# Second expert layer: where the gate product is read, where the overflow branch stands, and how the last norm is formed

## The chip, the cores and the metric

The kernel runs on one core of a Trainium2 chip, as one program. The metric is the time of the whole program in microseconds (us) on the device, as the median of three runs. Beside the runs there is one execution that the hardware profiler recorded; its trace is what the rows below come from. Engines are named as the profile names them: PE is TensorE (matmuls), PEld its weight loads, DVE VectorE, ACT ScalarE, POOL GpSimd, SP SyncE. SPq, POOLq and so on are the sequencers that issue DMAs.

## The reference, cut to what matters

The program is two transformer blocks on 256 tokens of width 1024. The change touches the last part of the second block, a layer of eight experts with a layer norm behind it:

```python
def _moe_swiglu(u, w_router, w_gate, w_up, w_down):      # u: 256 x 1024, 8 experts, top 2, inner width 2816
    ...
    h = silu(ragged_dot(xs, w_gate, group_sizes)) * ragged_dot(xs, w_up, group_sizes)
    ys = ragged_dot(h, w_down, group_sizes) * top_w[order]
    return segment_sum(ys, tok, num_segments=n_tok)

# second_block, layer 1
ff = _moe_swiglu(u, ...)
x = _layernorm(DEEPNORM_ALPHA * x + (1.0 + g2) * ff, ln2_g, ln2_b)   # the program's output
```

All weights and products are float32.

## The kernel before, in words

The program is written as a list of jobs that run in one order; each engine's instructions stand in the order in which the jobs record them. Semaphores between engines are set by the framework, tile by tile.

**Experts and slots.** `second_moe` visits the eight experts in the order 0, 5, 1, 2, 6, 3, 4, 7. `CAP` gives each a fixed number of token slots: 96 for experts 0 to 4, and 64 for 5, 6 and 7. So the second, fifth and eighth experts visited have 64 slots, and expert 7, the last, is one of them. Slots 0 to 63 are "part 0", slots 64 to 95 "part 1" (only where `CAP` is 96). The tokens of an expert are gathered with matmuls against a matrix of zeros and ones (`np`) into `nX`.

**Chunks.** An expert's inner width of 2816 is taken in six chunks (`c` = 0 to 5), five of 512 and one of 256. In each chunk, for each part, `proj_jobs` multiplies `nX` first with the gate weights (key "g2") and then with the up weights ("u2"). Both products lie side by side in one PSUM tile, `box[part]`, which is one bank. ACT takes silu of the gate half into `ns` (L1864), DVE multiplies it by the up half into `nH` (L1866). Then `down_jobs` multiplies the chunk before ("d2", from `nHT` into the accumulators `acc`), and only after that `turn` transposes this chunk's `nH` on TensorE (L286) and copies it to `nHT` (L1883). So the down product of one chunk is done between the projections and the transposes of the next. An expert's finished sums are weighted, spread back to the tokens by matmuls (`combine`, `rest`) and added to `x` by DVE while the next expert runs.

**Weights.** Each weight tile is 1 MB (128 partitions x 2048 floats). 264 of them are needed in this layer, and there are 14 slots for them. SP issues all their loads in the order of first use (L166); a load waits until TensorE has finished with the tile that held its slot before. SP is one queue: whatever stands ahead of a load holds it up.

**Overflow branch.** `many` handles tokens beyond the fixed slots. It begins with a branch on a count that every engine loads (L1031, L1032), SP included, and jumps over a long body when the count is zero, as it is in these runs. It is job `J(many)`; before, it stands in the last expert visited (`x == NE2 - 1`) at chunk 3, ahead of that chunk's `turn`. A similar branch stands in the first block's expert layer, at about 260 us.

**End.** `end` weights the last expert's sums (`nyA`, L1933), spreads them to the tokens by four matmuls into four PSUM banks, adds them to `x` in SBUF (L2092), and makes the layer norm of the two halves of the tokens (`x0`, `x1`): statistics on DVE (L310), square root on ACT, then scale and shift, shared by ACT, DVE and POOL for `x0` and done by DVE alone for `x1`. Four DMAs write the output. The rows of norm weights are broadcast by two POOL DMAs of 0.5 MB into the tile `nrow`, which shares its memory with a tile of the overflow body.

Of the kernel before, what the change touches and what calls it, by code (L numbers as in the profile page):

```python
# [15 lines left out]
AF = mybir.ActivationFunctionType  # L16
OP = mybir.AluOpType
AX = mybir.AxisListType

P = 128  # L20
SEQ = 256
D = 1024
KD = D // P
# [5 lines left out]
NE2 = 8  # L29
C2 = 128  # L30
FF2 = 2816
ALPHA = 4.0 ** 0.25
RMS_EPS = 1e-6
LN_EPS = 1e-5
# [76 lines left out]
class Build:  # L111
# [192 lines left out]

    def stats(self, x):

        n = x.shape[1] // 512
        st = self.sm([P, n, 6], "bn_st")
        for i in range(n):
            self.nc.vector.bn_stats(st[:, i, :], x[:, i * 512:(i + 1) * 512])  # L310
        return st

    def deviation(self, st, eps, rms):
# [1381 lines left out]
    def second_moe(self):  # L1695
        nc, I, J = self.nc, self.I, self.job
# [141 lines left out]
        def proj_jobs(p, c, box, part):  # L1838

            n = min(512, FF2 - c * 512)  # L1840
            nj, fw, nq = 2048 // n, n // 2, n // P
            m, at, w = (nq, 32, P) if part else (2, 64, fw)
            stride = P if part else 256
            for a, key in enumerate(("g2", "u2")):
                for half in range(KD // nj):
                    def run(t, a=a, half=half):
                        X = place[p]["X"][:, :, 64:96] if part else place[p]["X"][:, :, 0:64]
                        w3 = t.rearrange("p (j n) -> p j n", n=n)
                        if a == half == 0:
                            box[part] = self.ps()  # L1850
                        for jj in range(nj):
                            j = half * nj + jj
                            for q in range(m):
                                self.mm(box[part][at * q:at * q + at, a * stride:a * stride + w], X[:, j, :],
                                        w3[:, jj, q * w:(q + 1) * w], j == 0, j == KD - 1)
                        if half < KD // nj - 1:
                            return
                        if "H" not in box:
                            box["s"] = self.t([P, 384], "ns", bufs=2)
                            box["H"] = self.t([P, 384], "nH", bufs=2)  # L1860
                        r, dst = slice(0, at * m), slice(256, 384) if part else slice(0, fw)
                        src = box[part][r, a * stride:a * stride + w]
                        if a == 0:
                            nc.scalar.activation(box["s"][r, dst], src, AF.Silu)  # L1864
                        else:
                            nc.vector.tensor_mul(box["H"][r, dst], box["s"][r, dst], src)  # L1866

                    J(run, (key, p, c, half))

# [65 lines left out]
                                               op1=OP.mult)  # L1935
            eb["y"] = y

        def combined(p, eb):

            y, PT = eb["y"][0], eb["PT"]  # L1940
            out = [[self.ps("acc") for _ in range(2)], [self.ps() for _ in range(2)]]
            for t in range(2):
                for dh in range(2):
                    r = slice(64 * dh, 64 * dh + 64)
                    self.mm(out[t][dh], PT[r, 0, t * P:(t + 1) * P], y[r, :], True, True)
            return out

        def combine(p, eb):
            def run():
                out = combined(p, eb)  # L1950
                for t in range(2):
                    for h in range(2):
                        dst = self.x[t][:, h * 512:(h + 1) * 512]
                        nc.vector.tensor_add(dst, dst, out[t][h])

            def rest():

                out = [self.ps() for _ in range(4)]
                y, PT = eb["y"][1], eb["PT"]
                for t in range(2):  # L1960
                    for dq in range(4):
                        r = slice(32 * dq, 32 * dq + 32)
                        self.mm(out[dq][:, t * 256:(t + 1) * 256], PT[r, 1, t * P:(t + 1) * P], y[r, :], True, True)
                for dq in range(4):
                    for t in range(2):
                        dst = self.x[t][:, dq * 256:(dq + 1) * 256]
                        nc.vector.tensor_add(dst, dst, out[dq][:, t * 256:(t + 1) * 256])

            J(run)
            return rest  # L1970

        def many():
            def body(e, rk, w):
# [51 lines left out]
        for p in ORDER:  # L2025
            for c in range(NC):
                n = min(512, FF2 - c * 512)
# [15 lines left out]
        for x, p in enumerate(ORDER):  # L2043
            eb = {}
            for c in range(NC):
                box = {}

                for part in (0, 1) if kind == 0 else (1, 0):
                    if part == 0 or CAP[p] > 64:
                        proj_jobs(p, c, box, part)  # L2050
                        kind = part
                    if x == c == 0 and part == 0:
                        J(by_tokens)
                        J(lambda: self.settled(lambda _, c: c > 9))
                        J(spread_gate)
                    if prev is not None and (part == 0 or CAP[prev[0]] > 64):
                        down_jobs(*prev, part)
                        kind = part
                if x == NE2 - 1 and c == 3:
                    J(many)  # L2060
                if prev is not None and prev[0] != p:
                    J(lambda a=prev: self.chain.append(lambda: weighted(a[0], a[3])))
                    waiting = prev
                turn(p, c, box)
                if c == 0:
                    weights_of_slots(p, eb)
                if c == 1 and waiting is not None:
                    rest = combine(waiting[0], waiting[3])
                    waiting = rest if CAP[waiting[0]] > 64 else None
                if c == 2 and waiting is not None:  # L2070
                    J(waiting)
                    waiting = None
                if c == 3 and x < NE2 - 1:
                    J(lambda b=ORDER[x + 1]: self.chain.extend([lambda: places(b), lambda: None] + gather(b)))
                prev = (p, c, box, eb)
        down_jobs(*prev, 0)

        def end(p=prev[0], eb=prev[3]):

            half = [slice(h * 512, (h + 1) * 512) for h in range(2)]  # L2080
            r = self.t([P, 2, D], "nrow", tag="nrows")
# [1 line left out]
            self.bcast_row(rg, I["ln2_g_2"][1:2, :])  # L2083
            self.bcast_row(rb, I["ln2_b_2"][1:2, :])
            weighted(p, eb)
            ps = combined(p, eb)
            mv, r = self.t([P, 2, 2], "e_mv"), self.t([P, 2], "e_r")
            b = self.t([P, 1], "e_b")

            def added(t):  # L2090
                for h in range(2):
                    nc.vector.tensor_add(self.x[t][:, half[h]], self.x[t][:, half[h]], ps[t][h])  # L2092

            def moments(t):
                st = self.stats(self.x[t])
                nc.vector.bn_aggr(mv[:, t, :], st.rearrange("p a b -> p (a b)"))  # L2096
                nc.vector.tensor_scalar_add(r[:, t:t + 1], mv[:, t, 1:2], LN_EPS / ALPHA ** 2)  # L2097
                nc.scalar.activation(r[:, t:t + 1], r[:, t:t + 1], AF.Sqrt)

            x0, x1 = self.x  # L2100
            added(0)
            moments(0)
            added(1)
            nc.vector.reciprocal(r[:, 0:1], r[:, 0:1])
            nc.vector.scalar_tensor_tensor(out=b, in0=mv[:, 0, 0:1], scalar=-1.0, in1=r[:, 0:1], op0=OP.mult, op1=OP.mult)  # L2105
            for h in range(2):
                nc.scalar.activation(x0[:, half[h]], x0[:, half[h]], AF.Identity, scale=r[:, 0:1], bias=b)  # L2107
            moments(1)
            for h in range(2):
                nc.vector.tensor_mul(x0[:, half[h]], x0[:, half[h]], rg[:, half[h]])  # L2110
                nc.gpsimd.tensor_add(x0[:, half[h]], x0[:, half[h]], rb[:, half[h]])
                nc.sync.dma_start(self.out[0, 0:P, half[h]], x0[:, half[h]])
            nc.vector.reciprocal(r[:, 1:2], r[:, 1:2])
            for h in range(2):
                nc.vector.scalar_tensor_tensor(out=x1[:, half[h]], in0=x1[:, half[h]], scalar=mv[:, 1, 0:1],  # L2115
                                               in1=rg[:, half[h]], op0=OP.subtract, op1=OP.mult)
                nc.vector.scalar_tensor_tensor(out=x1[:, half[h]], in0=x1[:, half[h]], scalar=r[:, 1:2],  # L2117
                                               in1=rb[:, half[h]], op0=OP.mult, op1=OP.add)
                nc.scalar.dma_start(self.out[0, P:2 * P, half[h]], x1[:, half[h]])

        J(end)

# [34 lines left out]
```

## Time and profile before

| what | value |
|---|---|
| three runs | 2068.54, 2069.56, 2069.57 us; median 2069.56 us |
| the profiled execution: its own time, its span in the trace | 2069.82 us, 2068.1 us |
| TensorE busy over the span | 1881.0 us (91%) |
| DVE, ACT, POOL busy | 662.2 us (32%), 443.0 us (21%), 106.6 us (5%) |
| granted TensorE clock, mean over the span | 0.973 of full speed |
| read from HBM | 655.30 MB |

The second expert layer's matmuls run from about 1280 us to 2051 us, more than a third of the span; the norm and the output take the last 17 us. "Busy" of an engine counts its own instructions, not its waits. An idle stretch of an engine is given in square brackets with the event that ended it.

### The profile page before, as it was taken

To read this page: it belongs to the slowest core of one execution; us is meant where nothing else is said; L and a number is where in the kernel's file an instruction comes from. 1 tells how busy PE (TensorE), PEld (TensorE's weight loads), DVE (VectorE), ACT (ScalarE), POOL (GpSimd) and SP (SyncE) were. 2 spreads that over 40 slices of the span, in tenths; PEclk is the share of its full clock that TensorE was granted. 3 is DMA by queue.
4 is the path that set the end of the run, shared out by engine and by line. 5 is a ranking of instruction groups with operands and counts; after the bars stand their busy time and mean duration, and the time that the engine had idled before them with its cause. 6 is when DMAs were issued, how large, how long until landed. Compare 5 with 4: busy or idle time off the path is not lost. (4 is left out here: it accounts for less than half of the span.)

```text
span 2068.1 us, 42041 instructions
## 1 busy us (share of the span) xinstructions
PE 1881.0 (91%) x18649; PEld 1333.2 (64%) x18650; DVE 662.2 (32%) x1201; ACT 443.0 (21%) x718; POOL 106.6 (5%) x97
## 2 busy tenths in 40 slices
PE   4999889999999979989998998999999999999995
PEld 2989655555554548979996896665556555565652
DVE  6454621122211235655455564202110111111112
ACT  4544410000001024444343442000000000000000
POOL 7020200000000000000000001000000000000000
PEclk9999999999999999989998998999999999999998
DMA  9759989999999999357737846899999889998894
GB/s 369 291 212 315 347 304 386 394 393 393 393 395 394 393 379 368 123 184 266 264 122 255 315 146 243 296 346 391 392 368 346 326 329 390 393 384 305 315 394 160
DMA packets 293665, 660.78 MB, mean 320 GB/s; under 512 B 11320, under 2 KB 30928, under 8 KB 293216
## 3 DMA queue, kind: packets, MB, share of 16 engines
q1 hardware_dynamic: 290864, 648.46, 84.9%
q0 software_dynamic: 2320, 8.97, 1.1%
q8 instruction: 152, 2.49, 0.5%
q10 hardware_dynamic: 288, 0.52, 0.1%
q14 instruction: 41, 0.34, 0.0%
HBM read 655.30 MB, written 2.62 MB: 318 GB/s over the span
## 5 line engine op out<-in xcount | busy, mean ns | idle before, releaser
L289 PE MATMUL mm<-w,nX 128*32 128x128 f32 (+2 forms) x6592 | 446.7, 317 | 38.1 <-ACT ns L1864 32.3
L289 PEld LDWEIGHTS mm<-w,nX 128*32 128x32 f32 (+1 forms) x6592 | 307.1, 123 | 176.8 <-ACT ns L1864 57.6
L204 DVE TENSOR_TENSOR wh<-w,wh 128x1024 fp32r<-128x1024 f32 x178 | 222.6, 1257 | 171.2 <-ACT wh L208 166.8
L289 PE MATMUL mm<-w,mxt 128*64 128x256 f32 x2048 | 235.5, 383 | 21.9 <-ACT msg L1251 17.5
L289 PEld LDWEIGHTS mm<-w,mxt 128*64 128x64 f32 x2048 | 145.5, 138 | 119.6 <-ACT msg L1251 32.1
L289 PE MATMUL acc<-w,nHT 128*32 128x256 f32 (+1 forms) x1584 | 215.1, 474 | 2.5 <-issue 2.0
L208 ACT ACTIVATE wh<-w 128x1024 fp32r<-128x1024 f32 x178 | 184.6, 1043 | 103.8 <-PE acc L289 65.3
L289 PE MATMUL mm<-uh,wh 128*128 128x256 f32 (+1 forms) x1376 | 194.5, 292 | 11.7 <-ACT uh L302 8.9
L289 PEld LDWEIGHTS mm<-uh,wh 128*128 128x128 f32 (+1 forms) x1376 | 178.1, 196 | 18.6 <-ACT uh L302 12.3
L1866 DVE TENSOR_TENSOR nH<-ns,mm 128x256 f32<-128x256 f32 (+2 forms) x78 | 27.7, 356 | 467.4 <-PE mm L289 461.4
L1864 ACT ACTIVATE ns<-mm 128x256 f32<-128x256 f32 (+2 forms) x78 | 25.8, 331 | 638.3 <-PE mm L289 638.3
L289 PEld LDWEIGHTS acc<-w,nHT 128*32 128x32 f32 (+1 forms) x1584 | 79.5, 122 | 98.9 <-issue 78.8
L289 PE MATMUL mm<-w,mHT 128*64 128x512 f32 x512 | 116.9, 598 | 13.2 <-DVE mHT L1278 13.2
L289 PE MATMUL mm<-ul,wh 128*128 128x256 f32 (+1 forms) x688 | 101.2, 292 | 0.0
L289 PEld LDWEIGHTS mm<-ul,wh 128*128 128x128 f32 (+1 forms) x688 | 92.1, 197 | 1.1
L289 PEld LDWEIGHTS mm<-w,mHT 128*64 128x64 f32 x512 | 33.9, 136 | 74.9 <-issue 53.4
L1254 DVE TENSOR_TENSOR mH<-msg,mm 128x256 f32<-128x256 f32 x32 | 13.5, 421 | 206.2 <-PE mm L289 206.2
L289 PE MATMUL mm<-hh,wh 128*128 128x256 f32 x416 | 60.7, 296 | 7.4 <-ACT wh L208 6.7
L1296 DVE SCALAR_TENSOR_TENSOR mYl<-mm,mws,mYh 128x512 fp32r<-128x512 f32 x32 | 24.0, 751 | 135.2 <-ACT mYh L1295 135.2
L1295 ACT ACTIVATE mYh<-mm,mws 128x512 fp32r<-128x512 f32 x32 | 22.0, 687 | 201.0 <-PE mm L289 201.0
L289 PEld LDWEIGHTS mm<-hh,wh 128*128 128x128 f32 x416 | 55.7, 202 | 9.6 <-ACT wh L208 7.2
L357 POOL TENSOR_TENSOR x<-x,sv 128x512 f32<-128x512 f32 x10 | 12.6, 1277 | 840.6 <-DVE sv L356 840.6
(423 smaller groups left out, 1901.7 us busy)
## 6 DMA issues: line engine op xcount, KB each, us to landing
w<-in_moe_w_gate_dram SPq DMA_DIRECT2D x88, 1024.0 KB, 12.8
w<-in_moe_w_up_dram SPq DMA_DIRECT2D x88, 1024.0 KB, 13.6
w<-in_moe_w_down_dram SPq DMA_DIRECT2D x88, 1024.0 KB, 12.5
w<-in_w_gate_dram SPq DMA_DIRECT2D x64, 1024.0 KB, 15.3
w<-in_w_up_dram SPq DMA_DIRECT2D x64, 1024.0 KB, 14.6
w<-in_w_down_dram SPq DMA_DIRECT2D x64, 1024.0 KB, 14.0
w<-in_ada_w_dram SPq DMA_DIRECT2D x24, 2048.0 KB, 10.3
w<-in_w_in_dram SPq DMA_DIRECT2D x19, 2048.0 KB, 15.2
```

The lines of the kernel that those rows point to most:

```text
L204: nc.vector.tensor_sub(lo, src, hi.bitcast(F32))
L208: nc.scalar.activation(shaped(hi), src, AF.Copy)
L289: self.nc.tensor.matmul(out, lhsT=lhsT, rhs=rhs, start=start, stop=stop)
L357: nc.gpsimd.tensor_add(self.x[1][:, sl[h]], self.x[1][:, sl[h]], y[h])
L1254: nc.vector.tensor_mul(H, box["s"], ps[:, 256:512])
L1295: nc.scalar.activation(Yh, ps, AF.Copy, scale=box["ws"])
L1296: nc.vector.scalar_tensor_tensor(out=Yl, in0=ps, scalar=box["ws"], in1=Yh.bitcast(F32), op0=OP.mult, op1=OP.subtract)
L1864: nc.scalar.activation(box["s"][r, dst], src, AF.Silu)
L1866: nc.vector.tensor_mul(box["H"][r, dst], box["s"][r, dst], src)
```

## The change

Three edits, all in or behind the second expert layer.

1. In `proj_jobs`, silu of the gate product is no longer recorded after the gate's last matmul but after the up product's last matmul, just ahead of the multiplication.
2. `J(many)`, the overflow branch, moves from the eighth expert visited, chunk 3, to the fifth, chunk 4; in both it stands ahead of the chunk's `turn`.
3. A new job `carried`, after the eighth expert's chunk 3, multiplies `x` by the identity into the four PSUM banks that `end` will use. The last matmuls then add on top of it in PSUM (`start` false), so that the four additions in SBUF fall away; statistics and the first step of the norm read PSUM, and the second half of the tokens takes the same path as the first. POOL's two additions go to DVE.

```diff
     def stats(self, x):
-        n = x.shape[1] // 512
-        st = self.sm([P, n, 6], "bn_st")
-        for i in range(n):
-            self.nc.vector.bn_stats(st[:, i, :], x[:, i * 512:(i + 1) * 512])
+        if not isinstance(x, list):
+            x = [x[:, i * 512:(i + 1) * 512] for i in range(x.shape[1] // 512)]
+        st = self.sm([P, len(x), 6], "bn_st")
+        for i, h in enumerate(x):
+            self.nc.vector.bn_stats(st[:, i, :], h)
         return st
...
-                        if half < KD // nj - 1:
+                        if a == 0 or half < KD // nj - 1:
                             return
...
-                        src = box[part][r, a * stride:a * stride + w]
-                        if a == 0:
-                            nc.scalar.activation(box["s"][r, dst], src, AF.Silu)
-                        else:
-                            nc.vector.tensor_mul(box["H"][r, dst], box["s"][r, dst], src)
+                        gate, up = (box[part][r, b * stride:b * stride + w] for b in range(2))
+                        nc.scalar.activation(box["s"][r, dst], gate, AF.Silu)
+                        nc.vector.tensor_mul(box["H"][r, dst], box["s"][r, dst], up)
...
+        def banks():
+            return [[self.ps("acc") for _ in range(2)], [self.ps() for _ in range(2)]]
+
-        def combined(p, eb):
+        def combined(p, eb, out, start):
             y, PT = eb["y"][0], eb["PT"]
-            out = [[self.ps("acc") for _ in range(2)], [self.ps() for _ in range(2)]]
             for t in range(2):
                 for dh in range(2):
                     r = slice(64 * dh, 64 * dh + 64)
-                    self.mm(out[t][dh], PT[r, 0, t * P:(t + 1) * P], y[r, :], True, True)
-            return out
+                    self.mm(out[t][dh], PT[r, 0, t * P:(t + 1) * P], y[r, :], start, True)
...
+        def carried():
+            self.xs = banks()
+            for t in range(2):
+                for h in range(2):
+                    self.mm(self.xs[t][h], self.ident, self.x[t][:, h * 512:(h + 1) * 512], True, False)
...
-                if x == NE2 - 1 and c == 3:
+                if x == 4 and c == 4:
                     J(many)
...
+                if x == NE2 - 1 and c == 3:
+                    J(carried)
                 prev = (p, c, box, eb)
...
             weighted(p, eb)
-            ps = combined(p, eb)
...
+            xs = self.xs
+            combined(p, eb, xs, False)
+            first = self.deviation(self.stats(xs[0]), LN_EPS / ALPHA ** 2, False)
+            st = self.stats(xs[1])
+            moments = [first, None]
+            for t in range(2):
+                if t == 1:
+                    moments[1] = self.deviation(st, LN_EPS / ALPHA ** 2, False)
+                mv, r = moments[t]
+                nc.vector.reciprocal(r, r)
+                b = self.sm([P, 1], "bn_b")
+                nc.vector.scalar_tensor_tensor(out=b, in0=mv[:, 0:1], scalar=-1.0, in1=r, op0=OP.mult, op1=OP.mult)
                 for h in range(2):
-                    nc.vector.tensor_add(self.x[t][:, half[h]], self.x[t][:, half[h]], ps[t][h])
...
+                    x = self.x[t][:, half[h]]
+                    nc.scalar.activation(x, xs[t][h], AF.Identity, scale=r, bias=b)
+            for t in range(2):
+                for h in range(2):
+                    x = self.x[t][:, half[h]]
+                    nc.vector.tensor_mul(x, x, rg[:, half[h]])
+                    nc.vector.tensor_add(x, x, rb[:, half[h]])
+                    (nc.sync, nc.scalar)[t].dma_start(self.out[0, t * P:(t + 1) * P, half[h]], x)
```

TensorE's rows in the last expert's chunk 4, before the change, with the semaphores that each row waits for (`DMAHW` is a weight tile's landing, `Activation` is ACT). The rows with `w,nX` are the two gate tiles, then the two up tiles; those with `w,nHT` are the down product of chunk 3; L286 is `turn`.

```order
L289 MATMUL mm<-w,nX 64x256 [waits DMAHW6_49,PE_49,Activation_49]
L289 MATMUL mm<-w,nX 64x256 x7
L289 MATMUL mm<-w,nX 64x256 [waits DMAHW7_49]
L289 MATMUL mm<-w,nX 64x256 x7
L289 MATMUL mm<-w,nX 64x256 [waits DMAHW0_49,Activation_49]
L289 MATMUL mm<-w,nX 64x256 x7
L289 MATMUL mm<-w,nX 64x256 [waits DMAHW1_49]
L289 MATMUL mm<-w,nX 64x256 x7
L289 MATMUL acc<-w,nHT 64x512 [waits DMAHW2_49,DVE_49]
```

The same place after the change, with the two pairs of identity matmuls ahead of the gate.

```order
L289 MATMUL acc<-x_81,cst 128x512 x2
L289 MATMUL mm<-x_82,cst 128x512 x2
L289 MATMUL mm<-w,nX 64x256 [waits DMAHW6_49,Activation_49]
L289 MATMUL mm<-w,nX 64x256 x7
L289 MATMUL mm<-w,nX 64x256 [waits DMAHW7_49]
L289 MATMUL mm<-w,nX 64x256 x7
L289 MATMUL mm<-w,nX 64x256 [waits DMAHW0_49]
L289 MATMUL mm<-w,nX 64x256 x7
L289 MATMUL mm<-w,nX 64x256 [waits DMAHW1_49]
L289 MATMUL mm<-w,nX 64x256 x7
L289 MATMUL acc<-w,nHT 64x512 [waits DMAHW2_49,DVE_49]
```

The wait for ACT at the first up tile is gone; the one at the first gate tile stays. The matmuls of `carried` wait for nothing.

SP's queue around the branch, before the change: the last three weight loads, and behind them the branch (its body, not taken, is left out).

```order
L166 DMA w<-in_moe_w_down_dram 128x2x1024
L166 ISA
L166 DMA w<-in_moe_w_down_dram 128x2x1024
L166 ISA
L166 DMA w<-in_moe_w_down_dram 128x2x1024
L1031 TENSOR_LOAD rt_mi
L1031 ISA x2
L1032 COMPARE_AND_BRANCH
```

SP's queue after the change, the rows where the branch is left and the loads go on (behind its skipped body):

```order
L1035 COMPARE_AND_BRANCH
L1035 UNCONDITIONAL_BRANCH
L1033 UNCONDITIONAL_BRANCH
L166 ISA
L166 DMA w<-in_moe_w_down_dram 128x2x1024
L166 ISA
L166 DMA w<-in_moe_w_gate_dram 128x4x512
```

Before, no load stands behind the branch; now 90 of the 264 do. The first of them is the second down tile of the sixth expert's chunk 0.

## Rows read from the trace of the kernel before

**Rows 1.** Windows, fifth expert: stretch, its length, engines' busy us, clock, DMA share, GB/s.

```profile
1680.00:1753.00 73.00, 70.20 (x564) 39.36 (x563) 13.58 (x36) 4.30 (x11) 0.00 (x0) 1.00 1.04 390
```

**Rows 2.** Waits of PE from 1280.5 to 2050.9: total us, times, longest.

```profile
PE mm L289 <- ACT ns L1864: 32.3, 71, 1.5
PE mm L286 <- PEq L1032: 4.4, 1, 4.4
```

**Rows 3.** Timeline, last expert, chunk 2: start, us, engine, line, operation, records, idle before.

```profile
1993.83 3.67 PE L289 MATMUL mm<-w,nX 128*64 128x256 f32 x32
...
1997.55 0.38 ACT L1864 ACTIVATE ns<-mm 128x256 f32<-128x256 f32 x1 [13.10 <-PE mm L289]
...
1997.99 3.67 PE L289 MATMUL mm<-w,nX 128*64 128x256 f32 x32 [0.48 <-ACT ns L1864]
...
2001.49 3.60 PE L289 MATMUL acc<-w,nHT 128*64 128x512 f32 x16
2001.78 0.42 DVE L1866 TENSOR_TENSOR nH<-ns,mm 128x256 f32<-128x256 f32 x1 [6.23 <-PE mm L289]
```

**Rows 4.** Timeline, sixth expert, chunk 0: `turn` of part 1, and the next down product.

```profile
1767.30 0.29 DVE L1866 TENSOR_TENSOR nH<-ns,mm 128x128 f32<-128x128 f32 x1 [5.92 <-PE mm L286]
...
1767.64 0.33 PE L286 MATMUL mm<-cst,nH 128*128 128x128 f32 x1 [0.48 <-DVE nH L1866]
...
1773.26 1.91 PE L289 MATMUL acc<-w,nHT 128*32 128x256 f32 x32
```

**Rows 5.** Landing time of single loads, issued at 1368.89, 1465.60 and 1758.34 us.

```profile
w<-in_moe_w_down_dram SPq DMA_DIRECT2D x1, 1024.0 KB, 4.9
...
w<-in_moe_w_down_dram SPq DMA_DIRECT2D x1, 1024.0 KB, 13.7
...
w<-in_moe_w_down_dram SPq DMA_DIRECT2D x1, 1024.0 KB, 14.4
```

**Rows 6.** Timeline: single load issues, and the third expert's first down product.

```profile
1465.60 1.03 SPq L166 DMA_DIRECT2D w<-in_moe_w_down_dram  x1
...
1661.47 0.92 SPq L166 DMA_DIRECT2D w<-in_moe_w_gate_dram  x1
...
1758.34 1.02 SPq L166 DMA_DIRECT2D w<-in_moe_w_down_dram  x1
...
1481.18 1.47 PE L289 MATMUL acc<-w,nHT 128*32 128x256 f32 x22
```

**Rows 7.** Timeline of PE around the overflow branch, last expert, chunks 3 and 4.

```profile
2015.20 3.60 PE L289 MATMUL acc<-w,nHT 128*64 128x512 f32 x16
...
2023.69 2.82 PE L289 MATMUL mm<-w,nX 128*64 128x256 f32 x11
...
2036.63 3.60 PE L289 MATMUL acc<-w,nHT 128*64 128x512 f32 x16
...
2040.53 1.97 PE L289 MATMUL mm<-w,nX 128*64 128x128 f32 x32
```

**Rows 8.** Timeline of PE behind the first block's branch.

```profile
268.15 5.36 PE L289 MATMUL mm<-w,mxt 128*64 128x256 f32 x32 [4.19 <-DVEq L1032]
```

**Rows 9.** SP's waits from 2015 to 2040, then from 255 to 270.

```profile
SPq L1032 <- SPq L1032: 13.8, 2, 8.5
...
SPq L1032 <- SPq L1032: 5.0, 1, 5.0
```

**Rows 10.** Timeline of the end: additions, statistics, scaling, last steps.

```profile
2052.87 1.28 DVE L2092 TENSOR_TENSOR x<-x,acc 128x512 f32<-128x512 f32 x2 [1.22 <-PE acc L289]
2054.07 1.28 DVE L310 BATCH_NORM_STATS2 bn_st<-x 128x6 f32<-128x512 f32 x2
...
2057.28 1.52 ACT L2107 ACTIVATE x<-x,e_b,e_r 128x512 f32<-128x512 f32 x2 [1.26 <-DVE e_b L2105]
...
2058.80 1.29 DVE L2110 TENSOR_TENSOR x<-x,nrow 128x512 f32<-128x512 f32 x2
...
2064.13 0.75 DVE L2117 SCALAR_TENSOR_TENSOR x<-x,e_r,nrow 128x512 f32<-128x512 f32 x1
```

More of the change, by code (lines that the diff above doesn't have):

```diff
@@ L1944, in combined @@
                     r = slice(64 * dh, 64 * dh + 64)
-                    self.mm(out[t][dh], PT[r, 0, t * P:(t + 1) * P], y[r, :], True, True)
-            return out
+                    self.mm(out[t][dh], PT[r, 0, t * P:(t + 1) * P], y[r, :], start, True)
         def combine(p, eb):
             def run():
-                out = combined(p, eb)
+                out = banks()
+                combined(p, eb, out, True)
                 for t in range(2):
@@ L2085, in end @@
             weighted(p, eb)
-            ps = combined(p, eb)
-            mv, r = self.t([P, 2, 2], "e_mv"), self.t([P, 2], "e_r")
-            b = self.t([P, 1], "e_b")
-            def added(t):
-                for h in range(2):
-                    nc.vector.tensor_add(self.x[t][:, half[h]], self.x[t][:, half[h]], ps[t][h])
[L2094 to L2119, printed above, removed]
+            xs = self.xs
```

## Prediction

> **What bounds the kernel now.** I read the windows by expert first, then the waits of TensorE in the layer, then the timeline of one chunk, of the branch and of the end, and last the landing times of single weight loads. The window rows show the narrow balance of this layer: in the fifth expert, one of 64 slots, TensorE is busy for 70 of 73 us while the DMAs are full too, at 390 GB/s [rows 1]. The waits say that TensorE leads all the same. Between 1280.5 and 2050.9 us it waited 32.3 us for ACT's silu, in 71 waits of about 0.45 us, and 4.4 us at the overflow branch [rows 2]; no wait for a weight load of any size stands there. The chunk's timeline shows the repeated wait: gate matmuls, silu of 0.38 us, and the up matmuls, which start 0.48 us after the gate ended [rows 3]. They need nothing from silu; they only write the PSUM tile from which it reads.
>
> **Edit 1, gate read later.** The order of TensorE's rows shows the wait for ACT gone from the first up tile, so what it covers should go: **+32.3 us** [rows 2]. Ends: nothing, if another wait takes the same time, and all of it. I take all, since the matmuls that wait for nothing stand without a gap in the same timeline: the down product's 3.60 us start where the up matmuls end [rows 3].
>
> What silu did early it now does late: behind the up matmuls stand silu (0.38), the multiplication (0.42) and three handovers of some 0.1 us, about 1.1 us until `nH` is there. The cover is the down product of the chunk before, 3.60 us for part 0 [rows 3] and 1.91 us for part 1 [rows 4]. Only where a 96-slot expert follows one of 64, or nothing, does `turn` come straight behind part 1's projection; there its last transpose already waits 0.48 us for `nH` [rows 4]. Three such places (chunk 0 of the first, third and sixth experts), with silu's 0.28 us and a handover more at each: **-1.0 us**, at most 2.5 if the other first chunks wait too.
>
> **What is late next: the weights.** Earlier TensorE frees slots earlier, but the loads can't run faster than 390 GB/s, 2.69 us for a tile of 1 MB. A load issued at 1368.89 us landed after 4.9 us, so nothing was queued ahead of it; from there to the third expert the stream is back to back, and a load issued at 1465.60 took 13.7 us [rows 5, 6]. It landed at 1479.3. It holds the second half of the down product that starts at 1481.18 [rows 6], so it is used about 0.9 us later, at 1482.1: 2.8 us to spare. Up to 1369 us TensorE has dropped 10 of the 71 waits, one of them 1.5 us long: the stream starts some 5.3 us earlier. Up to 1482 it has dropped 22, some 10.7 us. So it now stands there for 10.7 - 5.3 - 2.8 = **-2.6 us**. Ends: 0, and 5 if the stream is not quite as dense.
>
> The same builds up before the sixth expert, where the load issued at 1758.34 landed 14.4 us later, at 1772.7, and was used in the second half of the product at 1773.26, about 1774.2: 1.4 us to spare [rows 4 to 6]. This is the very load that now stands first behind SP's branch.
>
> **Edit 2, the branch.** At the end it costs TensorE this: chunk 3's down product ends at 2018.80, the next gate starts at 2023.69, where one chunk later that step takes 0.30 us (2040.23 to 2040.53); and chunk 4 then runs 16.54 us from gate to down product's end [rows 7] where chunk 2 took 11.26 [rows 3]. Together 4.59 + 5.28 = **+9.9 us**, all on the path, since no weight is waited for there. In the fifth expert TensorE pays anew. Bounds: 5.9 us behind the first block's branch (4.19 idle, and 5.36 in place of 3.67 for the same matmuls) [rows 8, 3], and 9.9. I take **-9.9**, since there, as at the end, loads were streaming while the branch was passed.
>
> The Trainium skill's page "Runtime: NRT & Kernel Launch" (section on instruction fetch mechanics) says that a taken branch to a target outside the prefetched window stalls the engine for a fetch, so by it the branch costs at any place, which speaks against the move. By the larger row it gives 9.9 us back and takes 9.9; by the smaller one it would be 4.0 us better.
>
> SP pays too. It took 5.0 us over the first branch, and 13.8 in two waits over the last, the longer until all loads had landed [rows 9]. In the stream that means: behind load 173 no load is issued until the others have landed, then an idle queue's 4.9 us to the next landing [rows 5] in place of 2.69, some 3 us with the checks between. POOL's two row broadcasts, which need the branch passed, now fall into the same stretch: 1 MB, 2.7 us. So the stream loses about 6 us just where 1.4 were spare. The stream there begins with the issue at 1661.47 [rows 6], a wait for a slot; by then TensorE has dropped 40 waits, 18.2 us, less 2.6 and two of the three new waits for `nH`: 15 us earlier. At that load it has dropped 51, 23.2 us, less 3.6: 19.6. Without the branch it would come 3.3 us too soon for a stream that allows 15 + 1.4; with the branch it comes 9.7 us earlier, against 16.4 - 6 = 10.4. So TensorE's stall lets the weights catch up, and SP's stall hides behind it: **0**, with 0.7 us of room. If TensorE paid only 5.9 it would wait 3.3 there, so the smaller price brings 0.7 us, not 4.
>
> **Edit 3, the end.** The identity matmuls stand on TensorE's path in the last expert. A 512-column float32 pass takes 0.90 us: the down product's eight matmuls run in pairs, four passes in 3.60 us [rows 3]. Four full-width ones: **-3.6 us** (3.4 to 7.2, the latter if each needs two passes). `x` is long ready and the four banks are free, so nothing else waits.
>
> At the end DVE's chain from the first sums to its last step takes 2052.87 to 2064.88, 12.0 us. New: four statistics (2.6 us by [rows 10]), the small steps of the first half (0.3 each side of the root), ACT's scaling of it (1.52), the second root behind that on ACT, so that DVE's reciprocal waits for it until some 5.0 us, then 0.35 and eight multiplications and additions of 0.65 to 0.68: 10.8 us, **+1.2 us**. Ends 0 and 2: the additions go, but the chain still has to wait for the root in ACT's queue. DVE's additions from PSUM and its products from SBUF take the same 0.64 us [rows 10], so I put no price on reading PSUM. The Trainium skill's "Perfetto Trace Analysis" (section on optimizing Scalar/DVE operations) has a fixed cost of about 125 ns for DVE on PSUM against 60 on SBUF; by it the four statistics would take 0.26 us more and the sum would be 0.3 us worse.
>
> **Sum.** 32.3 - 1.0 - 2.6 + 9.9 - 9.9 - 3.6 + 1.2 = 26.3 us less than the profiled execution's 2069.82, which is 0.26 us over the median of the runs. So 2043.5, or against the median 2043.3 us.
>
> **Rivals.**
> - *The weights become the bound.* For: full DMAs and margins of 2.8 and 1.4 us. Against: only two short stretches have them. If SP's 5.0 us pass only after the loads have landed, TensorE waits 5.0 - 0.7 = 4.3 us more, and with the first shortfall at 5 the gain is 19.6: 2050 us.
> - *The other side: `turn` waits for the late silu.* If the down product did not cover the 1.1 us, each of 48 turns would pay it: 53 us, and the kernel would be 27 us slower, 2096 us. It decides from 0.55 us per turn on. Against: cover of 1.91 us or more at nearly all turns.
> - *Up still waits*, because the PSUM tile is held in some other way: no 32.3, no shortfall of 2.6 and no 1.0, so 2.4 us slower, 2072 us. Against: the order of rows.
> - *Everything goes well:* no shortfall (2.6), 0.7 at the branch, 2 at the end, no wait for `nH` (1.0): some 31 us, 2038.
>
> **How the numbers follow.** The forecast 0.70, weights 0.17, all well 0.04, up still waits 0.04, `turn` waits 0.05. A measurement of this kernel can tell about 0.2%, 4.1 us, from no change. The first three are faster (0.91), the fourth the same (0.04), the fifth slower (0.05). The range takes in the best case at its lower end; the upper end takes the weights' case with the dearer identity matmuls (3.6 more) and a late DVE end (1.2), and some for more stalls: 2038 to 2055.
>
> **What would show it.** PE's wait for `ns` gone from the list; a new wait for loads at the third expert's chunk 1, 2 to 3 us; a gap at the branch in the fifth expert, 4 to 5 us, and slow matmuls behind it; no more than about 1 us of new waits for `nH`; the last expert without a gap at chunk 3 and with 3.6 us of identity matmuls; DVE's last step some 10.8 us after the first sums in place of 12.0. Wrong if waits for loads sum to over 10 us, or if `nH` is waited for at most turns.

## The result, and the profile after

The changed kernel takes 2036.35 us (median of 4 runs, 2035.71 to 2039.49), the kernel before on the same chip 2069.05 us (4 runs): a ratio of 0.9846, 95% interval 0.9829 to 0.9863. The profiled execution has 2035.97 us, a span of 2034.2. The forecast was 2043.3 with a range from 2038 to 2055: the direction and the mechanism came out, the gain was 6 to 7 us larger than forecast, and the range missed the time by 1.7 us.

The waits of TensorE in the layer, 1279 to 2018.6 us (what waited, what it waited for, us in total, times, longest), to hold against [rows 2]:

```profile
PE mm L289 <- issue: 6.8, 5, 4.6
PE acc L289 <- DMA w<-in_moe_w_down_dram: 4.9, 3, 3.1
PE mm L286 <- PEq L1033: 4.1, 1, 4.1
PE acc L289 <- issue: 3.8, 2, 2.2
...
PE mm L286 <- DVE nH L1865: 1.7, 3, 1.0
```

No row for ACT's `ns` is left. In its place stand 4.9 us for weight loads, at the third expert, and 10.6 us of "issue", in which the engine waits for nothing that this list shows (5.7 us before); the last section says what these waits are.

The timeline of the last expert's chunk 2, which answers to [rows 3]:

```profile
1983.68 7.13 PE L289 MATMUL mm<-w,nX 128*64 128x256 f32 x64 [0.43 <-DVE x L1969]
...
1990.64 3.60 PE L289 MATMUL acc<-w,nHT 128*64 128x512 f32 x16
1990.85 0.38 ACT L1864 ACTIVATE ns<-mm 128x256 f32<-128x256 f32 x1 [12.62 <-PE mm L289]
...
1991.27 0.42 DVE L1865 TENSOR_TENSOR nH<-ns,mm 128x256 f32<-128x256 f32 x1 [5.66 <-ACT ns L1864]
```

Gate and up are now one row of 64 matmuls. From the first gate matmul to the down product it takes 6.96 us; before it took 7.66 (1993.83 to 2001.49). So 0.70 us went where the profile listed a wait of 0.48 between gate and up. `nH` is there at 1991.69, long before `turn` wants it behind the down product.

TensorE around the branch in the fifth expert, then the windows of the same stretch (from and to, length, busy us of PE, PEld, DVE, ACT and POOL with counts, granted clock, DMA share, GB/s):

```profile
1730.70 0.41 PE L286 MATMUL mm<-cst,nH 128*128 128x128 f32 x2 [4.05 <-PEq L1033]
1731.04 0.65 PE L289 MATMUL mm<-w,nX 128*64 128x128 f32 x6
1736.25 6.16 PE L289 MATMUL mm<-w,nX 128*64 128x128 f32 x57 [4.56 <-issue]
```

```profile
1726.00:1730.70 4.70, 0.65 (x4) 0.03 (x1) 0.00 (x0) 0.00 (x0) 0.05 (x1) 1.00 1.04 388
1730.70:1732.00 1.30, 0.99 (x8) 0.58 (x8) 0.42 (x1) 0.00 (x0) 0.99 (x2) 0.89 1.04 386
1732.00:1736.20 4.20, 0.00 (x0) 0.00 (x0) 0.00 (x0) 0.00 (x0) 0.00 (x0) 0.50 1.04 390
...
1738.00:1740.00 2.00, 2.00 (x24) 2.00 (x22) 0.00 (x0) 0.00 (x0) 0.00 (x0) 0.50 1.07 402
1740.00:1742.00 2.00, 2.00 (x22) 2.00 (x20) 0.00 (x0) 0.00 (x0) 0.00 (x0) 0.51 1.01 391
1742.00:1744.00 2.00, 2.00 (x17) 1.45 (x15) 0.29 (x1) 0.28 (x1) 0.00 (x0) 1.00 1.03 398
```

The branch has three prices here: 4.05 us of idle, 4.56 us of a second gap behind its first matmuls, and slow matmuls. The granted clock falls to 0.50, the lower of the two levels, behind the first idle stretch: it is there in the window of the second gap already (1732.00 to 1736.20) and stays there until about 1742 us. Meanwhile the DMAs go on at 386 to 402 GB/s: the weights catch up.

The end, which answers to [rows 10]:

```profile
2020.58 1.30 DVE L311 BATCH_NORM_STATS2 bn_st<-acc 128x6 f32<-128x512 f32 x2 [1.22 <-PE acc L289]
...
2022.22 1.29 DVE L311 BATCH_NORM_STATS2 bn_st<-mm 128x6 f32<-128x512 f32 x2
...
2023.80 1.45 ACT L2111 ACTIVATE x<-acc,bn_b,bn_r 128x512 f32<-128x512 f32 x2 [1.26 <-DVE bn_b L2108]
...
2030.35 0.69 DVE L2116 TENSOR_TENSOR x<-x,nrow 128x512 f32<-128x512 f32 x1
```

From DVE's first work on the sums to its last step: 2020.58 to 2031.04, 10.46 us in place of 12.0.

### The profile page after: what moved, and what is told of

It reads as the page before. It is cut to its first block, busy times and chain, and to the rows that moved or that the text cites. A ratio compares the mean times of both kernels' runs of the same rounds, so it can differ in the third digit from the quotient of the medians.

```text
span 2034.2 us, 41948 instructions
## 1 busy us (share of the span) xinstructions
PE 1870.9 (92%) x18657; PEld 1344.4 (66%) x18658; DVE 659.0 (32%) x1200; ACT 444.2 (22%) x720; POOL 103.4 (5%) x95
## 5 line engine op out<-in xcount | busy, mean ns | idle before, releaser
L289 PE MATMUL mm<-w,nX 128*32 128x128 f32 (+2 forms) x6592 | 434.7, 318 | 8.9 <-issue 6.8
L289 PEld LDWEIGHTS mm<-w,nX 128*32 128x32 f32 (+1 forms) x6592 | 317.2, 124 | 126.5 <-issue 36.8
L358 POOL TENSOR_TENSOR x<-x,sv 128x512 f32<-128x512 f32 x10 | 12.6, 1279 | 842.2 <-DVE sv L357 842.2
## 6 DMA issues: line engine op xcount, KB each, us to landing
w<-in_ada_w_dram SPq DMA_DIRECT2D x24, 2048.0 KB, 10.6
```

The costliest lines, as they stand in the source:

```text
L289: self.nc.tensor.matmul(out, lhsT=lhsT, rhs=rhs, start=start, stop=stop)
L358: nc.gpsimd.tensor_add(self.x[1][:, sl[h]], self.x[1][:, sl[h]], y[h])
```

## The experiments

All were timed in five rounds beside the kernel before (2068.2 to 2068.7 us in the three series). "From start to start" means the distance between the first matmuls of consecutive groups on TensorE, compared between two traces of the same order of groups. It needs no modelled end of a matmul. "The 78 steps" are those from the last gate group to the first up group of every chunk and part.

**1. The later silu alone** (`e1_gate_only`), **the branch alone** (`e2_branch_only`), **the end alone** (`e3_end_only`), **the first two** (`e4_gate_branch`). Each is the kernel before with that hunk of the change and no other.

```diff
 # e1: the two hunks of proj_jobs
-                        if half < KD // nj - 1:
+                        if a == 0 or half < KD // nj - 1:
...
 # e2: the place of the branch
-                if x == NE2 - 1 and c == 3:
+                if x == 4 and c == 4:
                     J(many)
...
 # e3: stats, banks, carried and end; e4: e1 and e2
```

> Edit 1 alone, branch and end as before. Theory S (a wait of TensorE costs its distance from start to start, about 0.6 us for each of 78 waits, 45 us in all): less some 9 us of new waits for loads before the third and the sixth expert, 36 us faster, about 2033 us. Rival L (a wait costs the idle time that the profile lists, 0.45 us for each of 71, 32 us in all, as in the prediction): 25 us faster, about 2044 us. In the trace S wants 6.9 to 7.0 us from gate to down product in a 64-slot chunk, in place of 7.66; L wants 7.2.

Measured: 2036.0 us (2034.4 to 2038.84), ratio 0.9844 (0.9831 to 0.9856). The later silu alone brings the whole gain. The 78 steps take 188.34 us in the kernel before and 143.22 here: 45.1 us less, where the profile had listed 32.3. In 70 of them something is gained, mostly 0.65 us for part 0 and 0.58 for part 1, where 0.48 and 0.40 were listed. (Up to the down product it is 0.05 more in part 0, the 0.70 above, since the up group behind a wait takes 3.50 us to the next start and otherwise 3.45.) New are the waits for loads, and one of 2.7 us for `nH` in the first expert:

```profile
PE acc L289 <- DMA w<-in_moe_w_down_dram: 9.5, 6, 2.8
PE mm L286 <- PEq L1032: 4.0, 1, 4.0
PE mm L286 <- DVE nH L1864: 3.4, 3, 2.7
```

> Edit 2 alone. The prediction's terms give 0 (9.9 saved at the end, 9.9 paid in the fifth expert). From the trace of the changed kernel, which shows some 11.3 us at the new place and 8.8 saved: 2 to 3 us slower, about 2071.5 us, since without edit 1 no wait for loads is there for the branch to hide. If the branch move were the source of the extra gain, it would be 5 us or more faster.

Measured: 2063.47 us (2059.18 to 2065.05), ratio 0.9971 (0.9961 to 0.9981): faster by about 5, against the expectation. Its last sentence takes 5 us or more as a sign that the branch is the source of the extra gain; e4 below settles this, since with the later silu the move gains nothing. The timeline at the new place:

```profile
1747.24 0.66 PE L286 MATMUL mm<-cst,nH 128*128 128x128 f32 x2 [4.08 <-PEq L1032]
1747.84 3.68 PE L289 MATMUL mm<-w,nX 128*64 128x128 f32 x32
1751.96 2.51 PE L289 MATMUL mm<-w,nX 128*64 128x128 f32 x32 [0.44 <-ACT ns L1864]
```

There is no second gap here. The two steps behind the branch lose 4.38 and 1.72 us, 6.1 in all (6.6 up to the next down product); at the end three steps give 4.59, 3.71 and 1.27 back, 9.6 (9.9 up to the down product). So the same instructions have no one price: it is 6.1 here, 9.6 at the end with a second gap of 2.19 us between the 11th and the 12th gate matmul behind the branch (the row of 11 at 2023.69 is the one ahead of it [rows 7]), and more in the changed kernel. Even the same place has two prices: with the later silu and the branch still at the end (e1) there is no second gap, and the branch costs 6.7 us up to the next down product. So some 3 us of e1's gain are the branch's, not the wait's.

> Edit 3 alone. The prediction's terms: 3.6 us for the identity matmuls, 1.2 back at the end, 2.4 us slower. From the trace of the changed kernel: 3.5 and 1.6, 1.9 us slower, about 2071 us. If edit 3 were the source of the extra gain, it would be 5 us or more faster.

Measured: 2067.78 us, ratio 0.9996 (0.9987 to 1.0005): no change, where some 2 us slower was expected. From the last down product to the end of the span it takes 15.67 us in place of 17.23, as forecast and a little more. The identity matmuls stand here right behind the branch, where the clock is low:

```profile
2022.98 0.66 PE L286 MATMUL mm<-cst,nH 128*128 128x128 f32 x2 [4.37 <-PEq L1033]
2023.43 3.62 PE L289 MATMUL acc<-x,cst 128*128 128x512 f32 x4
2026.85 2.90 PE L289 MATMUL mm<-x,cst 128*128 128x512 f32 x4
2029.68 3.67 PE L289 MATMUL mm<-w,nX 128*64 128x256 f32 x32
```

They take 6.25 us (2023.43 to 2029.68), but the gate matmuls behind them run at full speed, without the 2.19 us gap, and give 5.0 back (3.72 and 1.27).

> Edits 1 and 2 without edit 3. If edit 3 alone costs about 1.9 us, this is the changed kernel less 1.9: about 2034.5 us. If edit 3 pays for itself in this company, 2036.4 us or more.

Measured: 2036.53 us, ratio 0.9848 (0.9835 to 0.9861). No different from the later silu alone, nor from all three edits; the 2 us that the end was expected to cost (2034.5 without it) do not show in the medians. In the traces of e4 and the changed kernel they do: the identity matmuls cost 3.4 us, and the end gives 1.6 back. The waits for loads are 4.8 us in 3 times, as in the changed kernel, in place of 9.5 in 6: those ahead of the sixth expert are gone. In the trace, against e1 and from start to start, 11.6 us are paid at the branch, 8.7 us of load waits behind it come back, and 6.7 us at the end.

**2. The branch one expert later** (`e5_branch_sixth`).

```diff
 # the changed kernel
-                if x == 4 and c == 4:
+                if x == 5 and c == 4:
                     J(many)
```

> All three edits, but the branch one expert later (sixth, chunk 4). If the branch in the fifth expert pays for itself by letting the weights catch up, it comes too late here: the waits for weight loads ahead of the sixth expert come back (about 4.5 us, as edit 1 alone showed them) and the branch is paid on top (6 us, 11 with a fetch gap), so 2041 us, 2039 to 2047, with some 9 us of waits for w_down. If the branch costs the same wherever it stands, 2036 us and about 5 us of waits for w_down.

Measured: 2041.38 us (2038.24 to 2043.54), ratio 0.9861 (0.9845 to 0.9877). The waits for `w_down` are 9.4 us in 6 times again, those ahead of the sixth expert among them, and the branch is paid on top (6.7 us idle). So the place matters, by what the stall lets catch up.

**3. The wait taken away in another way** (`e6_two_tiles`): gate and up in two PSUM tiles, silu early as before.

```diff
 # the kernel before
-                        if a == half == 0:
-                            box[part] = self.ps()
+                        if half == 0:
+                            box[part, a] = self.ps()
...
-                                self.mm(box[part][at * q:at * q + at, a * stride:a * stride + w], X[:, j, :],
+                                self.mm(box[part, a][at * q:at * q + at, 0:w], X[:, j, :],
...
-                        src = box[part][r, a * stride:a * stride + w]
+                        src = box[part, a][r, 0:w]
```

> The kernel before, with the gate and the up product in two PSUM tiles in place of one; silu stays early, the branch and the end stay as before. It removes the wait in another way than edit 1. If a removed wait is worth the step from one matmul group's start to the next one's (0.60 to 0.70 us, 78 times, 45 us less some 9 us of new waits for loads): 2036 us, as edit 1 alone, or up to 3 us less since nH is not late. If it is worth what is listed (32.3 us less the same waits): 2045 us. If edit 1 gained because silu no longer reads the bank that the next matmuls write, the step shrinks here too; if because ACT and PE no longer work on PSUM at the same time at all, the step stays near 0.6 us longer and the time near 2060 us.

Measured: 2044.35 us (2044.24 to 2049.08), ratio 0.9892 (0.9877 to 0.9906). By the total this is the rival's number, but the steps speak for the first theory: the 78 steps give 45.09 us, to 0.03 the same as with the later silu. The wait was for the shared tile, and is worth the same however it goes; that ACT reads PSUM while TensorE writes another bank costs nothing there. What the profiled execution loses against e1 (5.6 us; the medians, from two series, differ by 8.3) stands elsewhere:

```profile
PE acc L289 <- DMA w<-in_moe_w_down_dram: 8.8, 6, 2.8
PE mm L289 <- issue: 7.7, 6, 3.2
PE mm L286 <- PEq L1032: 3.9, 1, 3.9
PE mm L286 <- DVE nH L1866: 3.1, 2, 2.6
PE acc L289 <- issue: 2.1, 2, 1.3
```

"issue" is 9.8 us here, 4.0 in e1: 3.2 us of it in one gap behind the branch at the end, the rest scattered over the layer. The last section says what these waits are and what sets the one behind the branch; why the scattered ones are longer in this kernel is not settled.

**4. The later silu for part 0 alone** (`e7_part0_only`).

```diff
 # the kernel before
-                        if half < KD // nj - 1:
+                        if (a == 0 and part == 0) or half < KD // nj - 1:
                             return
...
+                        if part == 0:
+                            gate, up = (box[part][r, b * stride:b * stride + w] for b in range(2))
+                            nc.scalar.activation(box["s"][r, dst], gate, AF.Silu)
+                            nc.vector.tensor_mul(box["H"][r, dst], box["s"][r, dst], up)
+                            return
```

> The kernel before with edit 1 for the slots of part 0 alone: 48 of the 78 places. By the step from start to start, 48 x 0.62 = 30 us less some 4 us of new waits for loads, about 2043 us, and the 30 places of part 1 keep their step of before. By the listed idle, 48 x 0.45 = 22 us less 1 or 2: 2048 us.

Measured: 2043.16 us (2041.19 to 2044.89), ratio 0.9876 (0.9861 to 0.9892). Its list of waits keeps one row for `ns`:

```profile
PE mm L289 <- ACT ns L1869: 13.1, 30, 1.5
```

So 19.2 listed us in 41 times went (32.3 - 13.1). The 48 steps of part 0 give 137.88 - 112.16 = 25.7 us; the 30 of part 1, where nothing is changed, take 52.65 us (50.46 before). Per listed microsecond that is 1.34 us, as in e1 (45.1 / 32.3 = 1.40).

**5. The later silu with the branch in the second expert** (`e8_branch_second`), **and all three edits with it there** (`e11_all_second`).

```diff
 # e8: e1 and this; e11: the changed kernel and this
-                if x == NE2 - 1 and c == 3:
+                if x == 1 and c == 4:
                     J(many)
```

> Edit 1, and the branch moved to the second expert, chunk 4, with the end as before. If the branch hides the load waits that follow it, those ahead of the third expert (about 5 us) go and those ahead of the sixth stay: net as with the branch in the fifth expert, 2036 us, 2034 to 2039. If the fifth place is the only one where it costs little, 2040 us: 6 to 11 us paid, 6 to 10 saved at the end, and 9 us of waits for w_down still there.

> All three edits with the branch in the second expert, chunk 4, in place of the fifth. The identity matmuls cost 3.5 us on the path and the end gives 1.6 back, so 2 us more than edit 1 with the branch in the second expert: 2035.6 us, with 9 us of waits for w_down. If the identity matmuls stand beside other waits and cost nothing: 2032 us.

Measured: e8 2033.69 us (2029.35 to 2034.17), ratio 0.9825 (0.9811 to 0.9838); e11 2036.59 (2034.69 to 2038.32), 0.9842 (0.9828 to 0.9857). In e8 the branch costs 4.16 + 1.02 = 5.2 us in the two steps behind it (5.8 up to the next down product), with no second gap, and the end gives back what the branch cost there: 9.6 against the kernel before, 6.7 against e1. But the waits for loads stay at 8.7 us, 4.3 of them in one wait at the third expert: SP waits 10.5 us at its own branch, the DMAs run dry from about 1475 to 1479 us (60, 0 and 51 GB/s in three slices of 1.4 us), and the first load behind, issued at 1477.28 and landed at 1482.19, is the one that the third expert waits for. So here the branch is cheap and hides no load. e11 differs from e8 by the end alone, and TensorE's row shows what the identity matmuls take where the clock is full:

```profile
1994.87 1.88 PE L289 MATMUL acc<-x,cst 128*128 128x512 f32 x4
1996.59 1.88 PE L289 MATMUL mm<-x,cst 128*128 128x512 f32 x4
1998.40 3.89 PE L289 MATMUL mm<-w,nX 128*64 128x256 f32 x34
```

3.53 us (1994.87 to 1998.40), against 1.55 that the end gives: edit 3 costs 2 us in the trace, 2.9 in the medians, which come from two series.

**6. No branch at all**, in the kernel before (`e9_before_no_branch`) and in the changed one (`e10_after_no_branch`): both leave out the handling of tokens beyond the fixed slots, by taking `J(many)` and the `if` above it out.

> The kernel before without the overflow branch (what it would do for tokens beyond the fixed slots is left out). If the branch at the end costs what the steps around it show (9.9 us in the profiled execution, all of it on the path since no load is waited for there): 2058.8 us. If only its 4.4 us of listed wait and the slower matmuls of about 1.5 us count, and the rest is fetching that comes anyway: 2062.7 us.

> All three edits without the overflow branch (its work for tokens beyond the fixed slots is left out). If TensorE's stall at the branch in the fifth expert lets the weights catch up, then without it the waits for w_down ahead of the sixth expert come back (from 4.9 to about 9.5 us listed, some 7 us from start to start) and only 4 us of the branch's 11 are gained: 2032 us, 2030 to 2034. If the branch's price simply adds to the rest: 2026 us.

Measured: e9 2057.99 us (2057.26 to 2064.53), ratio 0.9946 (0.9933 to 0.9959), some 10.6 us less than before; the same three steps as in e2 give 9.6. At the end of the layer the whole price is on the path. e10 2032.59 us (2029.41 to 2035.7), ratio 0.9825 (0.9809 to 0.9841). Three steps behind the former branch give 4.09, 6.24 and 1.42 back, 11.75 us, but TensorE's list from 1740 to 1800 us, empty of loads in the changed kernel, now reads:

```profile
PE acc L289 <- DMA w<-in_moe_w_down_dram: 3.8, 3, 1.6
PE mm L289 <- DMA w<-in_moe_w_up_dram: 2.2, 2, 1.6
```

So 11.75 come back and 6.0 listed, 7.05 from start to start, are lost again. The median is 3.8 us below the changed kernel's first one and 5.7 below the one that ran beside it (e12). A stall of 11.75 us in the stream costs 4 to 6, because the loads run on beneath it.

**7. The changed kernel once more** (`e12_again`).

> The changed kernel once more, beside the three others on the same chip: 2036.3 us, 2034 to 2039. If the gap of 4.6 us that followed the branch in the fifth expert (TensorE waiting for nothing that the profile shows) belongs to this order of the program, it is there again; if it wanders, it is gone or elsewhere.

Measured: 2038.33 us (2036.33 to 2038.78), ratio 0.9848 (0.9834 to 0.9862). The second gap is there again, at the same place:

```profile
1734.00 0.66 PE L286 MATMUL mm<-cst,nH 128*128 128x128 f32 x2 [3.94 <-PEq L1033]
1734.59 1.12 PE L289 MATMUL mm<-w,nX 128*64 128x128 f32 x6
1739.43 5.45 PE L289 MATMUL mm<-w,nX 128*64 128x128 f32 x57 [3.72 <-issue]
```

It came with 4.56, 4.4 (e4) and 3.72 us in three profiled executions of this place with the later silu, and not at all in e2, e8 and e11. So it belongs to an order of the program and not to chance; the last section shows what sets it.

## Why the prediction came out as it did

**The step that failed is the first one, "+32.3 us [rows 2]".** The mechanism was right: the wait is gone from every place and no other takes its time. The size was read from the wrong column, and the ground for taking it whole, that the down product starts "where the up matmuls end", misreads the rows. The idle that the profile lists before a matmul is counted from the modelled end of the one ahead, and consecutive groups of matmuls overlap by those ends: in [rows 3] the up group is 3.67 us long, but the down product starts 3.50 us after its start. A wait first uses up this 0.17 and only then shows as idle. So each listed 0.48 is 0.65 us of lost time, and 0.40 is 0.58; over 71 waits that is about 12 of the 12.8 us between 45.1 measured and 32.3 listed. The rest are a few steps that a stretch of lower clock or an "issue" wait made longer in one of the two traces. The rows for it stood in the prediction's own groups: 1993.83 to 1997.99 is 4.16 us, and the same 32 matmuls with no wait behind take 3.50. e1 and e7 show it in two doses, and e6 with the wait removed in another way.

**The late silu** was forecast at -1.0; the list of waits for `nH` went from 1.4 to 1.7 us (3.4 in e1 and e4, most of it one wait in the first expert). The down product covers it elsewhere, as argued.

**The weights at the third expert** were forecast at -2.6, at most 5. Listed are 4.9, from start to start 5.4 with the slower clock that follows. Since TensorE gains 1.4 times as fast as reckoned, it outruns the stream by more: with the prediction's own terms (10.7 - 5.3) x 1.4 - 2.8 = 4.8, so this follows from the first error.

**The branch at the end:** forecast +9.9, measured 9.6 in steps (e9, e2) and 10.6 in medians. **In the fifth expert:** forecast -9.9, measured 11.75 in steps (e10). The difference is in the main the second gap, 4.56 us there and 2.19 at the end. The prediction chose 9.9 over 5.9 because loads were streaming; this ground failed, since with loads streaming at 380 GB/s or more the branch cost 5.8 us in e8, 6.6 in e2 and 6.7 in e1. That the two prices nearly cancel, as forecast, is luck: each has a second gap. The Trainium skill's page "Runtime: NRT & Kernel Launch" (section on instruction fetch mechanics) has a taken branch to a target outside the prefetched window stall for a fetch; the traces agree in that every place paid, from 5.2 to 11.75 us.

**"TensorE's stall lets the weights catch up, and SP's stall hides behind it: 0"** held. No load is waited for at the sixth expert with the branch in the fifth; without it 6.0 us are listed (e10), 7.05 from start to start, where the prediction had 3.3 (again too little by the first error). SP's waits at its branch were 10.5 us in all, and none reached TensorE. That the branch should cost no more for being moved held with edit 1 (e4 against e1: the same) but not without it: alone, the move gained 5 us (e2), since then it is worth its difference in price (9.6 - 6.1 = 3.5 in the steps) and nothing has to catch up.

**The identity matmuls:** -3.6 forecast, 3.5 measured. **The end:** +1.2 forecast, 1.56 measured. The Trainium skill's page "Perfetto Trace Analysis" (section on optimizing Scalar/DVE operations) has a larger fixed cost for DVE on PSUM; here two statistics take 1.30 and 1.29 us from PSUM and 1.28 from SBUF [rows 10], so it does not show.

**The sum** with the measured sizes: 45.1 - 0.3 - 5.4 + 9.6 - 11.75 - 3.5 + 1.6 = 35.4 us. Layer and end became 32.2 us shorter (770.3 + 17.2 to 739.6 + 15.7). Of the missing 3, 2.5 are the growth of the "issue" waits other than those behind the branches (10.6 - 4.6 = 6.0 against 5.7 - 2.2 = 3.5); the largest two, 3.8 us together, stand within down products in the fourth expert. The list of terms is no exact account: the last gate step before the change, for one, stands in the 45.1 and in the 9.6. The layer also began 1.5 us earlier in this execution; nothing ahead of it is changed, and its start wanders between 1274 and 1283 us over the profiled executions.

**A better version?** The later silu with the branch in the second expert and the old end (e8) has the lowest median of the complete kernels, 2033.69 us; its slowest run, 2034.17, is below the fastest run of the changed kernel, 2035.71. The intervals of the two ratios overlap, and they ran in different series, so it is likely better by 2 to 4 us, not proven. Of the three edits the first makes the gain; with it in place the second is worth nothing at the place chosen, and the third costs about 2 us where it stands in the traces (e4 against the changed kernel, e8 against e11) and in one of the two pairs of medians.

## What to carry to other kernels

Price a repeated TensorE wait by the distance between matmul starts, with and without it, not by the idle time that the profile lists: here 0.65 against 0.48 us, 1.4 times. Before adding a stall to a stage whose loads are nearly late, ask what catches up meanwhile: 11.75 us of stall cost 4 to 6. And a stall taken out of the end of such a stage comes back whole (e9), since no load is left to be late. Where the list says "issue", look at the times of the instruction queue's packets (next section).

## What the runs showed of the hardware

**The "issue" waits end when a piece of TensorE's program has been loaded.** The profile has a DMA queue of kind "instruction", q8, whose packets are 16 KB each. The first row is its total in the changed kernel (packets, MB, share of the 16 DMA engines), the second the same for 1733 to 1735 us, inside the second gap behind the branch:

```profile
q8 instruction: 152, 2.49, 0.5%
...
q8 instruction: 1, 0.02, 3.5%
```

By the packet times in the trace this one runs from 1733.72 to 1734.83 us, and TensorE goes on at 1736.25, 1.4 us later. So it is everywhere: the fourteen traces have 80 "issue" waits of TensorE from the start of this layer on, and each ends 1.2 to 1.6 us behind the end of a q8 packet (of the 527 other waits there, 23 do). Counted in TensorE's records (matmuls, weight loads, semaphore waits), they stand multiples of 256 apart, within one record, in a trace and from trace to trace, with one shift, the same within three records, where the branch jumps over its body. So they stand at the ends of pieces, and a wait is what is missing when TensorE gets there.

That sets the second gap. Behind the branch the piece with its target is loaded, and the packet of the next piece starts 5.8 to 6.3 us after that one. What counts is how many records of the first piece are left behind the target:

| kernel | records left | second gap, us |
|---|---|---|
| changed kernel, e4, e12 | 17 | 4.56, 4.44, 3.72 |
| e6 | 21 | 3.16 |
| before | 27 | 2.19 |
| e7 | 55 | 0.86 |
| e1 | about 65 | none |
| e2, e5, e8, e11 | about 200 or more | none |

(In e3 it is 27 too, but 6.25 us of identity matmuls are among them, and there is no gap.) So an edit elsewhere can move a branch's price: edit 1 alone took the count at the old place from 27 to about 65, and the gap of 2.19 us was gone. No run changed the count alone.

A branch that every engine takes costs TensorE about 4.1 us of idle (6.7 in e5), and then a stretch at the lower clock: 0.50 granted from 1732 to 1742 us in the changed kernel, where the idle stretch of 4.05 us stood ahead and the one of 4.56 us lay inside. The same fall follows a wait for a load: around 3.07 and 1.39 us of idle at the third expert it goes to 0.50 in 1476.5 to 1479.0, and is at 1.00 again from 1481.

```profile
1474.00:1476.50 2.50, 1.11 (x20) 0.51 (x16) 0.00 (x0) 0.00 (x0) 0.00 (x0) 0.84 1.04 387
1476.50:1479.00 2.50, 2.50 (x20) 0.93 (x14) 0.00 (x0) 0.00 (x0) 0.00 (x0) 0.50 1.05 388
...
1481.00:1484.00 3.00, 3.00 (x30) 2.00 (x28) 0.00 (x0) 0.00 (x0) 0.00 (x0) 1.00 1.05 389
```

But in e10 waits of 1.62, 1.56 and 1.46 us in a row, ahead of the sixth expert, left it at 1.00 in all windows from 1755 to 1772. The prediction took the 5.28 us that chunk 4 lost behind the old branch from the rows, without their cause; it is the second gap of 2.19 us and the clock (0.50 in 2023.6 to 2026.0 and 0.51 in 2030.0 to 2032.0 of the kernel before).
